# First values ahead of the first keys, and the attention stage's first loads inside the last gate block, in a one-core hybrid attention and RG-LRU layer

## The chip, the core and the metric

The kernel is one program on one core of a Trainium2 chip. The time is the device time of one execution in microseconds (us), from launch to end. The core has five engines that this document names: TensorE (PE; the loading of its stationary operand is PEld), VectorE (DVE), ScalarE (ACT), GpSimd (POOL) and SyncE (SP), on whose queue nearly all DMA transfers are issued. Each engine runs its instructions in the order in which the program gives them; across engines they wait for one another by semaphores. TensorE's granted clock is shown as a share of full speed (1.00 is 2.4 GHz, 0.50 is 1.2 GHz).

## What is computed

One layer: a normalised and modulated input `h` (1152 tokens: 128 of context, 1024 latent) is projected by `w_in`; one part feeds differential attention, the other a recurrence run in both directions; each is gated, and both go through `w_out`. Cut to what matters:

```python
h = rms_norm(x, g_pre) * (1.0 + scale) + shift
p = h @ w_in
q, k, v, g_att, x_lru, g_lru = jnp.split(p, SPLITS, axis=-1)
if use_rope:
    q = axial_rope(q); k = axial_rope(k)
...
o = diff_attention(q, k_all, v_all, lam)          # 8 heads, two softmax maps each
att = (rms_norm(o, g_subln) * (1.0 - lam_init)).reshape(B, T, D_ATT) * jax.nn.silu(g_att)
u = centred_conv(x_lru, conv_w, conv_b)
a_f, b_f = lru_coeffs(u, w_r[0], b_r[0], w_i[0], b_i[0], lru_lam[0])   # two gates: a matmul and a sigmoid each
a_b, b_b = lru_coeffs(u, w_r[1], b_r[1], w_i[1], b_i[1], lru_lam[1])
hf = linear_scan(a_f, b_f, h0_f, False)
hb = linear_scan(a_b, b_b, h0_b, True)
lru = (hf + hb).astype(x.dtype) * jax.nn.silu(g_lru)
out = jnp.concatenate([att, lru], axis=-1) @ w_out
x_new = x + gate * rms_norm(out, g_post)
```

## The kernel before

All matrix work in single precision is done as three matmuls of split operands (`mm3`, lines 117 to 119: high by high, high by low, low by high). So each block of `w_in` is loaded (`wraw`, L257), copied by ScalarE to its high part (`whi`, L266), and GpSimd subtracts to get the low part (`wlo`, L114). `order` lists the blocks in the order of their use; loading and splitting run three blocks ahead of use. `wraw`, `whi` and `wlo` have two buffers each, the latter two for a pair of blocks.

The program has three stages. The **recurrence** goes over eight blocks `n` of 128 channels: projection and convolution, four gate matmuls (`ga<-uh,gwh`), and, one block late, the steps of block `p = n - 1`: `decays`, `gated`, `weights`, `roots` (square roots on ScalarE), `driven`, `scan` (L598, both directions), `both`, `mixed`, `mix_split` (L627 and L114, tiles `lmh` and `lml`), `mix_send` (stores to DRAM, `mix`). Block 7 has no successor, so its steps are put into the next stage.

The **projection stage** goes over four pairs of heads. A query or key block (`qk_block`) is three chunks of 24 matmuls into PSUM tiles, evacuated by ScalarE (L637); then `squares` (ScalarE, L768), `power` (a one-column matmul on TensorE, `un`, L779, and four tiny VectorE steps that make a power of two), `rope` (four VectorE steps, L751 to L754), `halves` (high half on ScalarE L794, low half on VectorE L795) and `send` (stores). A value block (`v_block`) is nine chunks of 24 shorter matmuls; after it `peak` and `spread` find a scale through two TensorE transposes (`vmt`, `vmu`) with VectorE steps between, and `halves` and `send` follow. Between the blocks' chunks `gate_step` sums up the modulation of the output (`gwhs`, `ghl`, and on TensorE `gacc`, L930). PSUM tiles of this kind (`small`) have five buffers. At the end come two gate blocks `g_block` (heads 6 and 7; sigmoid L606, product L612), and the pool `lp` of these stages is closed.

What is put between whose chunks is set by `tick()`, called after each chunk, and `after(d, fn)`, which runs `fn` `d` ticks later. Each `fn` only writes its instructions into the engines' queues at that place.

The **attention stage** runs over 72 tiles of queries (`period`): scores for two maps (`s`), maximum (DVE L1093), exponential (ACT L1103), combination (DVE L1121), transposes by DMA, product with values (`pv`); the matmuls of the output projection (`po<-woh,lt`) are dealt out among the periods by a table. Its first operands are the keys `kt`, queries `qt`, values `vt`, halves of `w_out` (`wor`, cast by `split_wo` to `woh` on ScalarE, L203, and `wol`, L114) and the left sides `lt`, read back from `mix`. Of `w_out` a half has 512 columns, and `GROUPS[0]` are the four rows of blocks 8 to 11.

## Time and profile before

| what | value |
|---|---|
| median of 3 runs | 1281.58 us (1278.58 to 1288.17) |
| the profiled execution, its own time | 1283.49 us |
| its span, first to last instruction | 1281.7 us |
| mean granted TensorE clock | 0.973 |
| busy: PE, PEld | 1174.4 us (92%), 1022.1 us (80%) |
| busy: DVE, ACT, POOL | 990.8 us (77%), 709.2 us (55%), 445.0 us (35%) |

The profile's span leaves out 1.8 us of the execution's time. In the profile's strip of 40 slices TensorE is nearly full up to the attention stage, except in two places, the slices from about 384 to 448 us and the slice from 737 us; the granted clock is below 1.00 in the same places. The recurrence ends at about 397 us, the projection stage at 749 us.

### The profile page before, as it was taken

Reading aid. Unit: us, or ns where it says so; the run is one execution under the profiler, and the core shown is the slowest. Engines: PE = TensorE matmul, PEld = TensorE weight load, DVE = VectorE, ACT = ScalarE, POOL = GpSimd, SP = SyncE. Lnnn points to the kernel's source line nnn. Section 1 sums busy time; section 2 is a strip of 40 time slices with the busy share of each in tenths; the row PEclk is TensorE's granted clock in tenths of the full one; section 3 lists DMA queues with packets and bytes.
Section 4 is the critical chain, followed back from the end, with each engine's and each line's share of the span. In section 5 each row is a group of like instructions: output and inputs, shape, how many; then the busy total and the mean of one; then the engine's idle time right before and its main releaser. Section 6 shows DMA issues by size and latency. Waiting matters only on the chain.

```text
span 1281.7 us, 19990 instructions
## 1 busy us (share of the span) xinstructions
PE 1174.4 (92%) x7704; PEld 1022.1 (80%) x7704; DVE 990.8 (77%) x1420; ACT 709.2 (55%) x1183; POOL 445.0 (35%) x228
## 2 busy tenths in 40 slices
PE   7899999999997899999999959988898887999787
PEld 1499999999997899998999956766666665667676
DVE  5938779777978946856768317899898989999977
ACT  4446545654665233433333327878777786777732
POOL 1421112111202122121122033346865577666724
PEclk8999999999998899999999979999999999999999
DMA  9221322223123634627435174989998988889864
GB/s 369 101 74 41 94 92 80 66 81 114 62 68 104 134 102 128 163 67 170 135 110 126 31 245 93 208 200 229 199 222 186 203 225 183 188 208 210 210 204 164
DMA packets 277815, 188.72 MB, mean 147 GB/s; under 512 B 196172, under 2 KB 246092, under 8 KB 276952
## 3 DMA queue, kind: packets, MB, share of 16 engines
q1 hardware_dynamic: 277432, 186.60, 55.5%
q8 instruction: 60, 0.98, 0.3%
q10 hardware_dynamic: 288, 0.85, 0.2%
q14 instruction: 35, 0.29, 0.1%
HBM read 102.20 MB, written 46.94 MB: 116 GB/s over the span
## 4 chain that ended last, share of the span: by engine, by line
PE 51%; DVE 26%; ACT 6%; DMA 6%; POOL 5%; issue 4%; SPq 1%; DVEq 0%; ACTq 0%; POOLq 0%
DVE mx L1093 5%; DVE e L1121 4%; PE ga L119 3%; PE ga L117 3%; PE ga L118 3%; DMA t<-a 3%; POOL a L1125 3%; PE v L117 3%; PE v L119 3%; PE v L118 3%; PE x L118 2%; PE x L119 2%; PE x L117 2%; PE g L117 2%; PE g L119 2%
## 5 line engine op out<-in xcount | busy, mean ns | idle before, releaser
L114 POOL TENSOR_TENSOR wlo<-wraw,whi 128x1024 fp32r<-128x1024 f32 x48 | 126.2, 2630 | 560.7 <-ACT whi L266 560.7
L1125 POOL TENSOR_TENSOR a<-e,a 128x1152 f16<-128x1152 f32 (+1 forms) x72 | 157.9, 2193 | 172.1 <-ACT a L1124 163.6
L1103 ACT ACTIVATE e<-s,mx,back 128x1152 f32<-128x1152 f32 (+1 forms) x144 | 175.5, 1219 | 67.9 <-DVE fa L1111 18.7
L1093 DVE TENSOR_REDUCE mx<-s 128x1 f32<-128x1152 f32 (+1 forms) x144 | 177.3, 1232 | 37.2 <-PE s L1086 36.5
L1084 PE MATMUL s<-kt,qt 128*128 128x384 f16 (+1 forms) x400 | 88.2, 325 | 41.8 <-ACT e L1103 40.3
L1121 DVE SCALAR_TENSOR_TENSOR e<-e,fa,e 128x1152 f32<-128x1152 f32 (+1 forms) x72 | 113.7, 1579 | 6.4
L117 PE MATMUL po<-woh,lt 128*128 128x512 f32 x216 | 100.1, 463 | 19.2 <-DMA lt<-mix 13.9
L117 PE MATMUL pv<-vt,t 128*128 128x128 f16 x584 | 102.5, 220 | 3.5 <-ACT ot L1140 2.0
L118 PE MATMUL pv<-vt,t 128*128 128x128 f16 x584 | 102.1, 220 | 0.0
L119 PE MATMUL pv<-vt,t 128*128 128x128 f16 x584 | 102.0, 220 | 0.0
L1124 ACT CAST a<-e 128x1152 f16<-128x1152 f32 (+1 forms) x72 | 75.8, 1053 | 36.8 <-DVE e L1121 24.5
L1084 PEld LDWEIGHTS <-qt 128*128 128x128 f16 x400 | 33.5, 97 | 72.1 <-issue 60.7
L1086 PE MATMUL s<-kt,qt 128*128 128x384 f16 (+1 forms) x400 | 87.9, 325 | 0.0
L119 PE MATMUL po<-woh,lt 128*128 128x512 f32 x216 | 87.3, 404 | 0.0
L118 PE MATMUL po<-wol,lt 128*128 128x512 f32 x216 | 87.3, 404 | 0.0
L117 PE MATMUL v<-whi,hTh 128*128 128x256 f32 x288 | 81.8, 284 | 0.0
L119 PE MATMUL v<-whi,hTl 128*128 128x256 f32 x288 | 81.5, 283 | 0.0
L118 PE MATMUL v<-wlo,hTh 128*128 128x256 f32 x288 | 81.5, 283 | 0.0
L117 PEld LDWEIGHTS <-t 128*128 128x128 f16 x584 | 57.3, 98 | 13.9 <-issue 8.9
L117 PEld LDWEIGHTS po<-woh,lt 128*128 128x128 f32 x216 | 42.3, 196 | 32.5 <-issue 14.3
L117 PE MATMUL k<-hTh,whi 128*128 128x384 f32 x192 | 67.4, 351 | 0.0
L117 PE MATMUL x<-hTh,whi 128*128 128x384 f32 x192 | 65.4, 341 | 2.1 <-DVE hTh L400 2.1
(329 smaller groups left out, 3604.7 us busy)
## 6 DMA issues: line engine op xcount, KB each, us to landing
wraw<-in_w_in_dram SPq DMA_DIRECT2D x48, 512.0 KB, 3.6
lt<-mix SPq DMA_DIRECT2D x27, 512.0 KB, 4.5
qs<-hlq SPq DMA_DIRECT2D x64, 144.0 KB, 3.1
qt<-qs SPq DMA_DIRECT2D x72, 128.0 KB, 4.0
wa<-in_w_ada_dram SPq DMA_DIRECT2D x16, 512.0 KB, 7.5
wor<-in_w_out_dram SPq DMA_DIRECT2D x32, 256.0 KB, 5.2
mix<-amo SPq DMA_DIRECT2D x6, 1152.0 KB, 5.1
ks<-hlk SPq DMA_DIRECT2D x32, 160.0 KB, 2.5
```

Source lines behind the costliest of these rows:

```text
L114: eng.tensor_tensor(out=lo, in0=val, in1=f(hi), op=ALU.subtract)
L117: PE.matmul(out, lhsT=lh, rhs=rh, start=start, stop=False)
L118: PE.matmul(out, lhsT=lh, rhs=rl, start=False, stop=False)
L119: PE.matmul(out, lhsT=ll, rhs=rh, start=False, stop=stop)
L1084: PE.matmul(sps[:, j, :w_], lhsT=qt[:, mp], rhs=kt_[:, mp, c], start=True, stop=False)
L1086: PE.matmul(sps[:, j, :w_], lhsT=qt[:, 2 + mp], rhs=kt_[:, mp, c], start=False, stop=True)
L1093: V.tensor_reduce(out=d["mx"][:, mp:mp + 1], in_=sv, axis=AX.XY, op=ALU.max, negate=True)
L1103: S.activation(out=e_[:, :nk].rearrange("p (j c) -> p j c", c=w_), in_=sv, func=AF.Exp, bias=d["mx"][:, mp:mp + 1], scale=unit, accum_out= ...
L1121: V.scalar_tensor_tensor(out=e1, in0=e1, scalar=d["fa"], in1=e0, op0=ALU.mult, op1=ALU.subtract)
L1124: S.copy(out=a16[:, 0:nk], in_=e1)
L1125: G.tensor_tensor(out=a16[:, nk:2 * nk], in0=e1, in1=a16[:, 0:nk], op=ALU.subtract)
```

## The change

Four things are moved; no arithmetic is added or taken away, except that two of the four low parts of each half of `GROUPS[0]` are now subtracted on VectorE in place of GpSimd. (1) In the first pair of heads the value block comes between the two query blocks and the two key blocks, and the weights are loaded in that order. (2) The steps of the recurrence's last block are spread over six ticks in place of four, and the steps of queries 0 and 1 (`squares`, `power` and `rope`, `halves`, `send`) are put at later ticks in the value block. (3) In all later blocks `rope` stands behind `power`, one tick later than before, and so do `halves` and `send`. (4) In the last gate block the loads are put in another order, `w_out`'s first halves are split before that block's sigmoids, and the second halves' loads and the first left side `lt` start there; the `lt` tiles move into the pool `kp`, and `load_lt` is defined earlier.

```diff
+    def load_lt(g, t):
+        lts[g, t] = kp.tile([P, 4, 2, P], F32R, tag="lt", name=f"lt{g}_{t}", bufs=4)
+        src = mixg[g][:, t] if g < 2 else mixg[g][:, :, :, t * P:(t + 1) * P]
+        move(out=lts[g, t].rearrange("p k s c -> p (k s) c"), in_=src.rearrange("p k s c -> p (k s) c"))
...
-            order += [(b + pr, m) for b in (0, 4, 8) for m in range(2)]
+            order += [(b + pr, m) for b in ((0, 4, 8) if pr else (0, 8, 4)) for m in range(2)]
...
         after(1, lambda: (weights(p, 0), weights(p, 1), roots(p)))
-        after(2, lambda: [f_(p, d) for d in range(2) for f_ in (driven, scan)] + [both(p)])
-        after(3, lambda: (mixed(p), mix_split(p), finish_state()))
-        after(4, lambda: mix_send(p))
+        after(2, lambda: (driven(p, 0), scan(p, 0)))
+        after(3, lambda: (driven(p, 1), scan(p, 1)))
+        after(4, lambda: (both(p), mixed(p)))
+        after(5, lambda: (mix_split(p), finish_state()))
+        after(6, lambda: mix_send(p))
...
-                junk = lp.tile([P, T + CTX], F32, tag="gs0" if early else "a", name=f"j{name}")
+                junk = lp.tile([P, T + CTX], F32, tag="a", name=f"j{name}")
...
+            def turned():
+                power()
+                rope(t_, name)
+
             def halves():
-                power()
-                d["hl"] = lp.tile([P, 2, T + CTX], F16, tag="gs2" if early else "w", name=f"hl{name}")
+                d["hl"] = lp.tile([P, 2, T + CTX], F16, tag="w", name=f"hl{name}")
...
-            if first:
-                after(1, lambda: (squares(), rope(t_, name)))
-                after(2, halves)
-                after(3, send)
-                return
-            for j in range(NCH):
-                qk_chunk(which, h, t_, j)
-                tick()
-            squares()
-            if which:
-                after(1, context_keys)
-            rope(t_, name)
-            after(1, halves)
-            after(2, send)
+            steps = [squares, turned, halves, send]
+            if not first:
+                for j in range(NCH):
+                    qk_chunk(which, h, t_, j)
+                    tick()
+            if which or h > 1:
+                squares()
+                if which:
+                    after(1, context_keys)
+                for x, step in enumerate(steps[1:]):
+                    after(1 + x, step)
+            else:
+                for x, step in zip(((7, 8, 10, 11), (8, 10, 12, 13))[h], steps):
+                    after(x - 3 * h, step)
...
         for pr in range(NH // 2):
-            for which in range(2):
-                for m in range(2):
-                    qk_block(which, 2 * pr + m)
-            v_block(pr)
+            for m in range(2):
+                qk_block(0, 2 * pr + m)
+            if pr == 0:
+                v_block(pr)
+            for m in range(2):
+                qk_block(1, 2 * pr + m)
+            if pr:
+                v_block(pr)
...
-        for n in range(4):
+        for n in range(2):
             load_q(n)
+        for kt in GROUPS[0]:
+            load_wo(kt, 0)
+        load_lt(0, 0)
+        after(2, lambda: [split_wo(kt, 0, V if kt % 2 else G) for kt in GROUPS[0][:2]])
+        after(3, lambda: [split_wo(kt, 0, V if kt % 2 else G) for kt in GROUPS[0][2:]])
+        after(3, lambda: [load_wo(kt, 1) for kt in GROUPS[0]])
+        g_block(gp_, NH - 1)
+        for n in range(2, 4):
+            load_q(n)
+        for t in range(1, 3):
+            load_lt(0, t)
         load_v(0)
         for kt in GROUPS[0]:
-            load_wo(kt, 0)
-        for h in range(len(AMONG) + 1, NH):
-            g_block(gp_, h)
-        for half in range(2):
-            for kt in GROUPS[0]:
-                split_wo(kt, half)
-                if half == 0:
-                    load_wo(kt, 1)
+            split_wo(kt, 1, V if kt % 2 else G)
         tick()
```

Three places of the new order matter below. **First**, ScalarE's queue behind the recurrence. Before, the squares of query 0 (`jq`) stand right behind the square roots of block 7 (`w`), and the wait for the power of two (`qksc`) stands in the first `hlq`:

```order
L637 ACTIVATE qfq_3165<-q_0_3166 128x384
L585 ACT_TABLE_LOAD
L585 ACTIVATE w_0_3196<-w_0_3196 128x1158
L585 ACTIVATE w_1_3199<-w_1_3199 128x1158
L768 ACTIVATE jq_3205,sqq_3204<-qfq_3024 128x1152
L637 ACTIVATE qfq_3165<-q_1_3212 128x384
L794 ACTIVATE hlq_3253<-qfq_3024,qksc 128x1152
L637 ACTIVATE qfq_3165<-q_2_3256 128x384
L768 ACTIVATE jq_3298,sqq_3297<-qfq_3165 128x1152
```

In the changed program these squares stand behind the fourth value chunk's copies (`vf<-v_3`); `jq` now takes a buffer that `lmh` had, of which the store must have landed:

```order
L644 ACTIVATE qfq_3165<-q_2_3234 128x384
L858 COPY vf_0_3264<-v_0_3269 128x128
...
L858 COPY vf_0_3264<-v_3_3374 128x128
L858 COPY vf_1_3265<-v_3_3374 128x128
L777 ACTIVATE jq_3404,sqq_3403<-qfq_3024 128x1152
L858 COPY vf_0_3264<-v_4_3406 128x128
L858 COPY vf_1_3265<-v_4_3406 128x128
L273 CAST whi_3300<-wraw_3193 128x1024
L777 ACTIVATE jq_3451,sqq_3450<-qfq_3165 128x1152
```

So six ticks' worth of TensorE work now lies between the roots and these squares. **Second**, ScalarE's queue where a sum of the output's modulation (`gwhs`) is cast for TensorE (`ghl`, read by `gacc`). Before, the cast stands behind the halves of a query (`hlq`), which wait for `rope`'s end on VectorE:

```order
L637 ACTIVATE qfq_4732<-q_0_4733 128x384
L794 ACTIVATE hlq_4773<-qfq_4620,qksc 128x1152
L637 ACTIVATE qfq_4732<-q_1_4776 128x384
L922 CAST ghl_4804<-gwhs_3980 128x512
L637 ACTIVATE qfq_4732<-q_2_4815 128x384
```

In the changed program it stands ahead of them:

```order
L644 ACTIVATE qfq_4727<-q_0_4728 128x384
L644 ACTIVATE qfq_4727<-q_1_4773 128x384
L936 CAST ghl_4801<-gwhs_3975 128x512
L806 ACTIVATE hlq_4804<-qfq_4620,qksc 128x1152
L644 ACTIVATE qfq_4727<-q_2_4807 128x384
```

On VectorE the sums of `gwhs` and the second subtraction of `ghl` likewise stand ahead of `rope` and `hlq`. **Third**, SyncE's queue at the last gate block. Before, four `qt`, `vt` and all eight loads of `w_out` stand ahead of the first left side:

```order
L969 DMA sgs_79<-sg_6268 128x1152
L210 DMA kt_6285<-ks 128x1280 x2
L219 DMA qt_0_6288<-qs_60 128x512
...
L219 DMA qt_3_6294<-qs_60 128x512
L214 DMA vt_6296<-vs_69 128x2560
L196 DMA wor_0_6298<-in_w_out_dram 128x512
...
L196 DMA wor_1_6410<-in_w_out_dram 128x512
L110 DMA lt_0_6442<-mix_81 128x1024
```

In the changed program two `qt` and the four first halves stand ahead of it, and `vt` comes last:

```order
L987 DMA sgs_79<-sg_6268 128x1152
L210 DMA kt_6285<-ks 128x1280 x2
L219 DMA qt_0_6288<-qs_60 128x512
L219 DMA qt_1_6290<-qs_60 128x512
L196 DMA wor_0_6292<-in_w_out_dram 128x512
...
L196 DMA wor_0_6298<-in_w_out_dram 128x512
L110 DMA lt_0_6300<-mix_81 128x1024
L196 DMA wor_1_6393<-in_w_out_dram 128x512
...
L110 DMA lt_2_6414<-mix_81 128x1024
L214 DMA vt_6416<-vs_69 128x2560
```

What moved there is the first left side, past the four second halves, of which each load waits until the split of a first half has freed its buffer.

## Rows read from the trace of the kernel before

**Rows 1.** Two stretches: busy PE, PEld, DVE, ACT, POOL, then clock, DMA share, GB/s.

```profile
480.00:700.00 220.00, 213.97 (x1350) 209.42 (x1349) 153.91 (x241) 79.92 (x141) 43.95 (x16) 0.98 0.50 130
1000.00:1200.00 200.00, 175.59 (x1428) 129.85 (x1427) 186.85 (x283) 149.48 (x281) 138.13 (x71) 0.98 0.90 206
```

**Rows 2.** TensorE's timeline, matmuls after idling: start, length, and [idle <-releaser].

```profile
383.77 0.45 PE L117 MATMUL ga<-uh,gwh 128*128 128x386 f32 x1 [2.12 <-ACT gs L561]
...
411.95 0.59 PE L779 MATMUL unq<-sqq,onesf 128*128 128x1 f32 x2 [6.47 <-ACT jq L768]
427.45 0.59 PE L779 MATMUL unq<-sqq,onesf 128*128 128x1 f32 x2 [4.73 <-ACT jq L768]
...
763.18 0.77 PE L117 MATMUL po<-woh,lt 128*128 128x512 f32 x1 [13.95 <-DMA lt<-mix]
```

**Rows 3.** Stretches around the two waits for `jq`, columns as in rows 1.

```profile
405.50:412.00 6.50, 0.04 (x1) 0.05 (x1) 5.50 (x6) 6.48 (x9) 3.08 (x1) 0.79 0.14 39
412.00:414.00 2.00, 2.00 (x7) 2.00 (x8) 1.97 (x2) 0.28 (x1) 0.00 (x0) 0.50 0.34 139
...
416.00:418.00 2.00, 2.00 (x12) 2.00 (x12) 2.00 (x2) 0.00 (x0) 0.00 (x0) 0.97 0.00 0
...
433.00:434.00 1.00, 1.00 (x7) 1.00 (x6) 1.00 (x1) 0.00 (x0) 0.00 (x0) 0.90 1.36 204
```

**Rows 4.** VectorE's timeline, steps of block 7 and of queries.

```profile
394.93 0.76 DVE L627 CAST lmh<-lsg 128x1152 fp32r<-128x1152 f32 x1
...
406.41 1.37 DVE L577 SCALAR_TENSOR_TENSOR w<-w,gs 128x1158 f32<-128x1158 f32 x1
...
413.19 1.23 DVE L754 TENSOR_TENSOR qfq<-qfq,rsq 128x1024 f32<-128x1024 f32 x1
...
416.07 2.32 DVE L598 TENSOR_TENSOR_SCAN w<-a,vec,gs 128x1024 f32<-128x1024 f32 x1
...
428.55 2.84 DVE L627 CAST lmh<-lsg 128x1152 fp32r<-128x1152 f32 x1
```

**Rows 5.** ScalarE's timeline: squares of query 0; a value chunk's two copies.

```profile
410.66 1.15 ACT L768 ACTIVATE jq<-qfq 128x1152 f32<-128x1152 f32 x1
...
720.77 0.43 ACT L844 COPY vf<-v 128x128 f32<-128x128 f32 x2 [2.45 <-PE v L119]
```

**Rows 6.** Chain that ended last, store of block 6: start, length, what.

```profile
395.72 3.79 DMA mix<-lmh
```

**Rows 7.** GpSimd's timeline: the weight split that the first value chunk will need.

```profile
406.92 3.08 POOL L114 TENSOR_TENSOR wlo<-wraw,whi 128x1024 fp32r<-128x1024 f32 x1 [18.80 <-ACT whi L266]
```

**Rows 8.** TensorE's waits from 480 to 740 us: total, times, longest.

```profile
PE gacc L930 <- ACT ghl L922: 3.5, 2, 2.2
PE gacc L930 <- DVE ghl L114: 1.5, 2, 0.8
```

**Rows 9.** Chain that ended last, transfers ahead of the attention stage.

```profile
738.48 4.59 DMA sgs<-sg
...
746.78 5.67 DMA wor<-in_w_out_dram
...
756.60 6.45 DMA lt<-mix
```

**Rows 10.** ScalarE's timeline, from the last sigmoid to the second tile's exponential.

```profile
749.14 0.49 ACT L606 ACTIVATE sg<-ga 128x384 f32<-128x384 f32 x1 [3.67 <-PE ga L119]
...
758.91 0.62 ACT L203 CAST woh<-wor 128x512 fp32r<-128x512 f32 x1 [0.29 <-DMA wor<-in_w_out_dram]
...
760.84 0.46 ACT L1103 ACTIVATE e<-s,mx,back 128x128 f32<-128x128 f32 x1
...
768.35 0.59 ACT L1044 COPY acc<-po 128x512 f32<-128x512 f32 x1 [6.96 <-PE po L119]
...
771.16 1.32 ACT L1103 ACTIVATE e<-s,mx,back 128x1152 f32<-128x1152 f32 x1 [1.55 <-DVE fa L1111]
```

**Rows 11.** VectorE's timeline: two low parts of `w_out` beside two on GpSimd.

```profile
1215.92 3.37 DVE L114 TENSOR_TENSOR wol<-wor,woh 128x512 fp32r<-128x512 f32 x2
```

More of the change, by code (lines that the diff above doesn't have):

```diff
@@ L219, in load_q @@
         nc.sync.dma_start(out=qts[h, i], in_=qs[h][:, i])
+    lts = {}
+    def load_lt(g, t):
+        lts[g, t] = kp.tile([P, 4, 2, P], F32R, tag="lt", name=f"lt{g}_{t}", bufs=4)
+        src = mixg[g][:, t] if g < 2 else mixg[g][:, :, :, t * P:(t + 1) * P]
+        move(out=lts[g, t].rearrange("p k s c -> p (k s) c"), in_=src.rearrange("p k s c -> p (k s) c"))
     with ExitStack() as pa:
@@ L759, in qk_block @@
             w_ = T + CTX if which else T
-            first, early = (which, h) == (0, 0), (which, h) < (0, 2)
+            first = (which, h) == (0, 0)
             t_ = blk["q0"] if first else lp.tile([P, T + CTX], F32, tag="u", name=f"qf{name}")
@@ L976, in hybrid_step_kernel @@
         kp = ctx.enter_context(tc.tile_pool(name="kp", bufs=2, side="right", reuse_waits="tile"))
-        gp_ = pa.enter_context(tc.tile_pool(name="gp", bufs=2, reuse_waits="tile"))
+        gp_ = pa.enter_context(tc.tile_pool(name="gp", bufs=1, reuse_waits="tile"))
         for n in range(2):
             load_k(0, n)
-        for n in range(4):
+        for n in range(2):
             load_q(n)
+        for kt in GROUPS[0]:
[4 more added lines that the diff above has]
+        after(3, lambda: [load_wo(kt, 1) for kt in GROUPS[0]])
+        assert len(AMONG) + 2 == NH
+        g_block(gp_, NH - 1)
[3 more added lines that the diff above has]
+            load_lt(0, t)
         load_v(0)
         for kt in GROUPS[0]:
-            load_wo(kt, 0)
-        for h in range(len(AMONG) + 1, NH):
-            g_block(gp_, h)
-        for half in range(2):
-            for kt in GROUPS[0]:
-                split_wo(kt, half)
-                if half == 0:
-                    load_wo(kt, 1)
+            split_wo(kt, 1, V if kt % 2 else G)
         tick()
@@ L998, in hybrid_step_kernel @@
         op = pb.enter_context(tc.tile_pool(name="op", bufs=1, reuse_waits="tile"))
-        first_lt = [op.tile([P, 4, 2, P], F32R, tag="lt", name=f"lt0_{t}", bufs=4) for t in range(3)]
         acc_o = [op.tile([P, D], F32, name=f"acc{t}") for t in range(NT)]
@@ L1006, in small @@
             return psb.tile([P, 512], F32, tag=tag, name=name, bufs=1)
-        lts = {}
-        def load_lt(g, t):
-            lts[g, t] = first_lt.pop(0) if first_lt else op.tile([P, 4, 2, P], F32R, tag="lt", name=f"lt{g}_{t}", bufs=4)
-            src = mixg[g][:, t] if g < 2 else mixg[g][:, :, :, t * P:(t + 1) * P]
-            move(out=lts[g, t].rearrange("p k s c -> p (k s) c"), in_=src.rearrange("p k s c -> p (k s) c"))
         def load_lt_pair(ts):
-            tile_ = op.tile([P, 2, 4, P], F32R, tag="lt", name=f"lt3_{ts[0]}", bufs=4)
+            tile_ = kp.tile([P, 2, 4, P], F32R, tag="lt", name=f"lt3_{ts[0]}", bufs=4)
             for a, t in enumerate(ts):
@@ L1278, in hybrid_step_kernel @@
             if i < 3:
-                before(-1, (lambda k=k: load_lt(*k)))
+                assert k == (0, i)
                 continue
```

## Prediction

> **What bounds the kernel now.** I read the strip of 40 slices first: it shows two stages with different limits. Up to the attention stage TensorE is the bound (213.97 of 220 us busy, VectorE 153.91); in the attention stage VectorE is (186.85 of 200), with TensorE idle an eighth of the time and the DMA engines 0.90 busy [rows 1]. So before 749 us the change is worth what it does to TensorE's waits, and afterwards what it does to the moment at which the attention stage starts to flow. Then I listed TensorE's waits by their place. Two long ones stand in the first slices of the projection stage, 6.47 and 4.73 us, both for the squares of a query; one of 13.95 us stands before the first `po` matmul, for a left side `lt` [rows 2]. A third view, the waits of TensorE between them, has only the four for `ghl` of any size, 3.5 and 1.5 us in all [rows 8]. The change touches all three places.
>
> A wait costs more than its length where the clock falls. The granted clock is 0.50 (1.2 GHz) after the 6.47 us wait and back near full only in the stretch from 416 us; after the second wait it rises in the stretch from 433 us [rows 2, 3]. TensorE worked through 4.0 us and some 5.7 us at half clock, which lost 2.0 and 2.9 us. The 2.12 us wait at 383.77 us was followed by matmuls at the usual pace: that matmul is 0.45 us long and those behind it lie 0.17 us apart [rows 2].
>
> **Part one: the queries' squares.** Removed: 6.47 + 4.73 + 2.0 + 2.9 = 16.1 us. The cause was VectorE and ScalarE, which had block 7's steps and both queries' steps at once, while TensorE had only three chunks of work between them. With the value block there, TensorE has nine chunks of 2.88 us (0.43 + 2.45, the distance of two evacuations [rows 5]) before it needs the keys.
>
> What takes its place, step by step:
> - The value block needs the low part of its second weights, which GpSimd has ready at 406.92 + 3.08 = 410.0 us [rows 7]. TensorE comes there at 405.5 us (where it began to wait for `jq`) and one chunk of 4.16 us (0.49 + 3.67 [rows 10]), at 409.7. A wait of 0.3 us.
> - Query 0's squares now stand behind the store of block 7's high part. VectorE ends `weights` at 407.8 [rows 4], waits for the roots, which ScalarE ends where `jq` starts before, at 410.7, the first of them about 1.1 us sooner, and does `driven` and `scan` twice: two times 1.37 + 0.4 + 2.32 (the short scan of the context taken as a sixth of the long one) [rows 4] is 8.2, to 418.3 from 410.1. Then `both` and `mixed` (1.4 each), two pairs of value maxima (an estimate of 0.5 a pair: twice a ninth of a 1.37 us step, and its start), and the cast at 0.76 us: 422.9. The store took 3.79 us in block 6 [rows 6], so it lands at 426.7; the squares take 1.15 and the read of the sum some 0.2 [rows 5]: 428.0. TensorE reaches `un` of query 0 after five value chunks, 410.0 + 14.4 = 424.4. A wait of 3.6 us.
> - `rope` of query 0 (about 5 us, four steps of the size of [rows 4]), `halves` (2.7, a step on ScalarE and one on VectorE) and the same for query 1 follow on VectorE from 428.6, about 8.5 us each with the maxima between, and then the last maxima: 448. TensorE ends the value block and the first key chunk at 428.4 + 11.5 + 4.2 = 444.1 and then wants `vm` for its transpose. A wait of some 3.6 us.
> - The first key's `un` follows the value's two high halves on ScalarE (two steps somewhat longer than `jq`, 2.6) and its own squares: 0.5 us by the same count.
>
> That is 0.3 + 3.6 + 3.6 + 0.5 = 8.0 us, net 16.1 - 8.0 = **8 us gained** if these waits leave the clock at full. They lie between the one that did (2.12) and the ones that did not (4.73), nearer to the latter; each fall would cost 2 to 3 us by the stretches above. So the term is 8, with 2 as the lower end (both fall, and 1 us more of wait) and 14 as the upper (the waits mostly go because a VectorE step or two comes sooner). I take 7, one half of a fall. The lower end has a reason too: the cast took 2.84 us, not 0.76, where a GpSimd split ran beside it [rows 4].
>
> The Trainium skill ("SBUF — State Buffer", the section "SBUF: two separate sides") says that VectorE and GpSimd share one pair of ports as an exclusive lock, so that the later one blocks for the whole instruction. The two casts agree (0.76 alone, 2.84 beside a split). By this rule alone the splits of `w_out` dealt to both engines would take turns; in the last part of the kernel, where they already are, two on VectorE took 3.37 us beside two on GpSimd [rows 11], and with that the term of part three loses under 1 us.
>
> **Part two: the cast of `gwhs`.** TensorE waits 2.2 and 1.3 us for the cast on ScalarE and twice about 0.8 us for the subtraction on VectorE, 5.0 us in all [rows 8]. In the new order the cast stands ahead of the `hlq` that waits for `rope`, and the subtraction ahead of the low half. VectorE's `rope` itself is now behind the sums, so the subtraction comes at about the old time less the two steps that went past it. I take 4 us, bounds 0 and 5. In the same blocks `rope`, `halves` and `send` come one chunk later. VectorE is busy 70% of this stage [rows 1], its steps for a block (about 8 us) fit in the 12.5 us of three chunks, and the tile they read is wanted again only two blocks on: nothing, with the case below as its price if that cover is gone.
>
> **Part three: the start of attention.** Before, `lt` lands after all of SyncE's queue: gate store until 743.1, `w_out`, then `lt` 6.45 us [rows 9]. Now `kt` and two `qt` (2.0 and 0.9 us of issue from 738.85) let the first `wor` go at 741.7. A load lands 5.7 us on by the chain [rows 9], so 747.4; the fourth is issued after the gate store has landed, 743.1, and lands at about 748.8; its cast ends at 749.4 (0.62 [rows 10]). `lt`, right behind, lands at 743.5 + 6.45 = 750.0. The three sigmoids of head 7 now stand behind these four casts: instead of being spread out they run together after 749.4, 1.3 us, and their products, half a microsecond each, end at 751.3, which the first `po` also needs. So TensorE starts `po` at 751.3 in place of 763.18, with a wait of about 2 us, and at full clock its twelve matmuls end at 754.
>
> The attention stage is not held by TensorE, though. The second halves of `w_out` stand on ScalarE ahead of the first exponential, each load waiting for a split: issue 749 to 750.5, landing 3 to 5.7 us later, the last cast over at 754 to 757. From that cast's start to the first exponential's start passed 1.93 us, and from the first `po`'s copy (768.35) to the first full-width exponential 2.81 us (771.16) [rows 10]. The first exponential thus starts at 755.5 to 758, the copy about 0.7 later, and the full-width one follows at 759 to 761.5. Against 771.16 that is 9.7 to 12 us; I take **11**. If the loads come as late as the old ones did behind four `qt` and `vt`, half of it remains (5); if the second halves land in 3 us, 13. The moved `vt` is first needed four periods on. `lt` in another pool has the same four buffers: nothing. What is gained here stays, because the later periods follow each other in a chain.
>
> **Sum.** 7 + 4 + 11 = 22 us. The profiled execution took 1283.49 us, so 1261.5 by its own time; it lies 1.9 us above the median of the runs shown, and from the median, 1281.58, the forecast is **1259.6 us**.
>
> **Rivals.**
> 1. *The new waits are as bad as the old.* Query 0's squares wait for a store, and `vm` for two queries' steps; if the cast meets a split and the clock falls twice, part one gives 1 us and the sum 16: 1265.6. For it speaks that the waits I count are 3.6 us; against, that they are shorter than both that lowered the clock. Chance 0.15. The Trainium skill ("TensorE: Matmul & The Clock Gate", "HAM oscillation — how this bites in real kernels") describes this, an engine that idles again and again and starts at half clock each time; the stretches here agree for 4.73 us and longer.
> 2. *The loads do not begin earlier in effect.* The queue's order changes, but the gate store and the DMA engines hold `wor` and `lt`; the first `po` would start at about 759 and the exponential at 768. Part three gives 3, the sum 14: 1267.6. Against it: `lt`'s 6.45 us counts from an issue that needs no split any more. Chance 0.10. That the change does less still, parts two and three nothing, leaves 7: 1274.6, chance 0.06.
> 3. *Slower: the later `rope` and `halves` hold up the projection stage.* Place: each of the twelve query and key blocks of pairs 1 to 3. VectorE's low half now ends a chunk later, and the block after next needs the tile that it reads; ScalarE would stand at that evacuation and TensorE after five PSUM tiles. It decides where VectorE ends `halves` more than a chunk (4.16 us) behind its place; then each block costs about one wait of 3 us, 36 us in all, against 22 gained: 1295.6. Against it: 30% of idle time on VectorE in this stage [rows 1]. Chance 0.04.
>
> **How the numbers follow.** The forecast case has 0.65; its own range is from 1247 (14 + 5 + 13 = 32 gained, and 2 us for the runs' spread) to 1268 (2 + 0 + 11 gained). Rivals 1 and most of 2 lie inside it. With the two rarer cases left out and a microsecond or two on the upper side, the range is 1248 to 1271. About 1%, 12.8 us, is what a measurement of this kernel can tell from no change. Faster by over 1% means under 1268.8: nearly all of the forecast, rival 1, and half of rival 2, 0.84; within 1% the rest of these and the case of 1274.6, 0.12; slower 0.04.
>
> **What would show it.** In the changed profile: TensorE's waits for `jq` or `vmt` together 5 to 10 us between 397 and 475 us, with no stretch at 0.50; the first query chunk of pair 1 starting at about 470 us in place of 478; no wait of `gacc` over 1 us; the first `po` at about 740 (751.3 less the 11 us gained before it) at clock 1.00, its wait about 2 us; the span of the attention stage as before. The prediction is wrong if VectorE cannot finish block 7 and the queries within the value block, if the second halves of `w_out` land later than 746 on the new time line (757 on the old), or if the attention stage gives the head start back because its DMA traffic, not its chain, sets its pace.

## The result and the profile after

The changed kernel takes 1262.59 us (median of 4 runs, 1259.25 to 1264.33) beside 1281.45 us for the kernel before: ratio 0.984, 95% interval 0.9814 to 0.9866. It ran once more, as a control among the experiments, at 0.9836 (0.9809 to 0.9863). The profiled execution took 1259.25 us with a span of 1257.5, against 1283.49 us before.

TensorE's waits in the first part of the projection stage, of the changed kernel (total, times, longest):

```profile
PE unq L788 <- ACT jq L777: 4.9, 1, 4.9
PE ga L117 <- ACT gs L568: 2.1, 1, 2.1
PE vmt L877 <- DVE vm L870: 1.9, 1, 1.9
PE v L118 <- POOL wlo L114: 0.3, 1, 0.3
```

The two waits for `jq` before [rows 2] are now one, and `vmt` has a wait of its own: 7.1 us without the old one of `ga`, where 11.2 stood. The same view from 470 to 740 us, where four waits of 5.0 us in all for `ghl` were [rows 8], and two of 0.8 us in all for `unk`:

```profile
PE unk L788 <- ACT jk L777: 2.2, 1, 2.2
PE gacc L944 <- DVE ghl L114: 1.2, 1, 1.2
```

Four stretches around the two waits in the value block (columns as in rows 1) answer to [rows 3]:

```profile
424.70:429.60 4.90, 0.02 (x2) 0.02 (x1) 1.84 (x5) 1.33 (x4) 0.00 (x0) 1.00 0.83 233
429.60:433.50 3.90, 3.90 (x20) 3.90 (x21) 3.65 (x9) 2.35 (x5) 2.39 (x1) 0.56 0.05 14
447.30:449.50 2.20, 0.25 (x3) 0.12 (x2) 1.93 (x4) 1.24 (x2) 1.27 (x1) 1.00 0.00 0
449.50:453.50 4.00, 4.00 (x16) 4.00 (x16) 1.11 (x5) 0.00 (x0) 1.39 (x1) 0.61 0.33 107
```

The clock falls behind both, also behind the one of 1.9 us. At 0.56 and 0.61 the two stretches lose 3.90 x 0.44 = 1.7 and 4.00 x 0.39 = 1.6 us.

Why `jq` waits: VectorE's timeline with block 7's two context scans (128 columns) and the cast whose store `jq` waits for ([rows 4] before), GpSimd's split beside it, and `jq` on ScalarE:

```profile
411.38 0.42 DVE L605 TENSOR_TENSOR_SCAN w<-a,gs 128x128 f32<-128x128 f32 x1
...
415.41 2.51 DVE L605 TENSOR_TENSOR_SCAN w<-a,gs 128x128 f32<-128x128 f32 x1
...
423.63 0.75 DVE L634 CAST lmh<-lsg 128x1152 fp32r<-128x1152 f32 x1
...
449.09 0.17 DVE L870 TENSOR_REDUCE vm<-vmx 128x2 f32<-128x20 f32 x1
```

```profile
414.68 2.95 POOL L114 TENSOR_TENSOR wlo<-wraw,whi 128x1024 fp32r<-128x1024 f32 x1 [4.55 <-ACT whi L273]
```

```profile
428.27 1.16 ACT L777 ACTIVATE jq<-qfq 128x1152 f32<-128x1152 f32 x1 [5.98 <-DMA mix<-lmh]
```

The first scan of 128 columns took 0.42 us, the second 2.51, until GpSimd's split was over at 417.63.

The start of the attention stage ([rows 2, 10] before), on TensorE, ScalarE and VectorE in this order:

```profile
740.44 0.73 PE L117 MATMUL po<-woh,lt 128*128 128x512 f32 x1 [2.94 <-DVE sg L619]
...
747.65 1.12 PE L1099 MATMUL s<-kt,qt 128*128 128x384 f16 x3 [2.48 <-ACT e L1118]
```

```profile
743.78 0.62 ACT L203 CAST woh<-wor 128x512 fp32r<-128x512 f32 x1 [0.51 <-DMA wor<-in_w_out_dram]
...
747.06 0.46 ACT L1118 ACTIVATE e<-s,mx,back 128x128 f32<-128x128 f32 x1
...
747.51 0.57 ACT L1059 COPY acc<-po 128x512 f32<-128x512 f32 x1
...
751.53 1.32 ACT L1118 ACTIVATE e<-s,mx,back 128x1152 f32<-128x1152 f32 x1 [3.00 <-DVE fa L1126]
```

```profile
744.43 0.74 DVE L114 TENSOR_TENSOR wol<-wor,woh 128x512 fp32r<-128x512 f32 x1 [1.90 <-ACT woh L203]
745.09 0.28 DVE L1108 TENSOR_REDUCE mx<-s 128x1 f32<-128x128 f32 x1
```

The clock under these `po` matmuls (a stretch, columns as in rows 1):

```profile
740.00:744.00 4.00, 3.56 (x9) 2.82 (x10) 2.08 (x4) 2.09 (x4) 1.94 (x2) 0.57 0.75 235
```

The wait of 13.95 us for `lt` is gone; 2.94 us for the last gate product stand there. Behind it the clock is 0.57. The first maximum follows VectorE's last subtraction for the second `w_out` halves, and the first full-width exponential comes at 751.53 in place of 771.16.

### The profile page after: what moved, and what is told of

Its sections match the earlier page's. It is cut to its first block, busy times and chain, and to the rows that moved or that the text cites. A ratio compares the mean times of both kernels' runs of the same rounds, so it can differ in the third digit from the quotient of the medians.

```text
span 1257.5 us, 19998 instructions
## 1 busy us (share of the span) xinstructions
PE 1166.2 (93%) x7704; PEld 1016.0 (81%) x7704; DVE 979.8 (78%) x1424; ACT 709.3 (56%) x1183; POOL 439.3 (35%) x224
## 4 chain that ended last, share of the span: by engine, by line
PE 55%; DVE 23%; ACT 6%; POOL 5%; DMA 5%; issue 4%; SPq 1%; DVEq 0%; ACTq 0%; POOLq 0%
DVE mx L1108 6%; DVE e L1136 4%; PE ga L119 3%; PE ga L117 3%; PE ga L118 3%; POOL a L1140 3%; PE x L118 2%; PE x L119 2%; PE x L117 2%; PE g L119 2%; PE k L117 2%; PE g L117 2%; PE g L118 2%; PE k L119 2%; PE k L118 2%
## 5 line engine op out<-in xcount | busy, mean ns | idle before, releaser
L114 POOL TENSOR_TENSOR wlo<-wraw,whi 128x1024 fp32r<-128x1024 f32 x48 | 123.1, 2566 | 552.0 <-ACT whi L273 552.0
L1108 DVE TENSOR_REDUCE mx<-s 128x1 f32<-128x1152 f32 (+1 forms) x144 | 177.4, 1232 | 21.8 <-PE s L1101 20.8
L117 PE MATMUL po<-woh,lt 128*128 128x512 f32 x216 | 98.4, 456 | 8.1 <-DVE acc L1065 3.3
L119 PE MATMUL po<-woh,lt 128*128 128x512 f32 x216 | 86.1, 398 | 0.0
L118 PE MATMUL x<-hTl,whi 128*128 128x384 f32 x192 | 65.3, 340 | 1.7 <-DVE hTl L114 0.9
```

The costliest lines, as they stand in the source:

```text
L114: eng.tensor_tensor(out=lo, in0=val, in1=f(hi), op=ALU.subtract)
L117: PE.matmul(out, lhsT=lh, rhs=rh, start=start, stop=False)
L118: PE.matmul(out, lhsT=lh, rhs=rl, start=False, stop=False)
L119: PE.matmul(out, lhsT=ll, rhs=rh, start=False, stop=stop)
L1108: V.tensor_reduce(out=d["mx"][:, mp:mp + 1], in_=sv, axis=AX.XY, op=ALU.max, negate=True)
```

## The experiments

Eleven kernels and the control. Two marks were read from each profile: the start of the last gate matmul (end of the projection stage) and of the first full-width exponential (attention flows); the last column is the time from there to the 126th such exponential. A third mark takes out how far an execution has come when it reaches the part that was edited: the matmul behind the 2.12 us wait for `gs` [rows 2], which stands ahead of all edits and comes between 383.77 and 386.96 us in these profiles. The fourth column is the time from it to the last gate matmul.

| kernel | ratio to before, 95% | last `ga` | from the wait for `gs` | first wide `e` | to the 126th |
|---|---|---|---|---|---|
| before | 1 | 748.76 | 364.99 | 771.16 | 425.26 |
| changed | 0.984 (0.9814 to 0.9866) | 737.04 | 353.19 | 751.53 | 420.43 |
| control: changed again | 0.9836 (0.9809 to 0.9863) | 738.41 | 353.46 | 752.83 | 427.23 |
| start put back | 0.9934 (0.9919 to 0.9949) | 741.80 | 356.56 | 763.55 | 425.22 |
| rope put back | 0.9873 (0.9856 to 0.989) | 742.89 | 357.75 | 757.23 | 424.27 |
| order put back | 0.9884 (0.9857 to 0.9911) | 744.72 | 360.31 | 758.86 | 428.10 |
| start alone | 0.9916 (0.9894 to 0.9937) | 750.57 | 365.14 | 764.48 | 424.14 |
| splits late | 0.9889 (0.9864 to 0.9914) | 738.21 | 353.16 | 755.50 | 425.22 |
| own buffer | 0.9799 (0.978 to 0.9818) | 734.74 | 347.91 | 748.77 | 420.53 |
| own buffer, peak late | 0.9757 (0.9735 to 0.978) | 729.30 | 343.90 | 742.64 | 421.96 |
| compact | 0.9822 (0.9799 to 0.9845) | 737.46 | 353.55 | 750.95 | 422.68 |
| compact, own buffer, peak late | 0.9755 (0.9737 to 0.9773) | 730.83 | 343.87 | 744.09 | 420.50 |
| second halves late | 0.9853 (0.9829 to 0.9876) | 737.18 | 353.14 | 747.17 | 424.48 |
| all mends | 0.9787 (0.9765 to 0.9809) | 729.19 | 343.89 | 741.84 | 429.26 |

A difference of two ratios counts in microseconds of 1282; the changed kernel is taken at 0.9838, the mean of its two. With intervals of 0.002 to 0.003 on either side, a difference is uncertain by 3 to 4 us. The fourth column is finer: it lies between 353.14 and 353.55 in the five profiles whose projection stage has the same edits or differs by the compact form alone, and between 343.87 and 343.90 in the three with both mends. It holds each profile's chance clock falls too, and says nothing of what comes behind it.

**Control.** 

> The changed kernel without an edit, beside the others on the same chip, so that differences of a few us can be told. Its ratio to the kernel before was 0.984 with an interval of 0.005; every theory expects the same, 0.984.

It came out so, by the ratio. The profiled execution is the longest of its five (1267.33 us, the others 1258.98 to 1260.84), and the marks put its excess behind the first wide exponential: 427.23 us to the 126th, 420.43 in the other profile of this kernel.

**Start put back.** The hunks on the attention start reversed (with them the gate blocks' pool, which has one buffer in place of two in the changed kernel).

> The changed kernel with the attention start put back as it was before the change (w_out, queries and left sides loaded behind one another, splits behind the last gate block); parts one and two stay. Forecast's term for part three, 11 us: 1262.6 + 11 = 1273.6 us. By the profile after, in which the first full-width exponential came 19.6 us earlier of which 11.7 already at the last gate matmul, the part is worth 7.9: 1270.5. Rival (attention is bound by its own flow and a later start is caught up there): under 1265.

0.9934, so by the ratio part three is worth 0.0096 x 1282 = 12.3 us, and attention does not catch up. The wait is back, on TensorE's timeline:

```profile
531.27 0.59 PE L781 MATMUL unk<-sqk,onesf 128*128 128x1 f32 x2 [2.21 <-ACT jk L770]
...
755.80 0.77 PE L117 MATMUL po<-woh,lt 128*128 128x512 f32 x1 [13.54 <-DMA lt<-mix]
```

The first of these rows is another matter: the changed kernel has the same wait of 2.21 us, with the same work around it, and in its two profiles the clock stayed. First the stretch of this kernel behind the wait, then that of the changed one:

```profile
530.00:536.00 6.00, 4.73 (x22) 4.73 (x23) 5.46 (x13) 2.65 (x6) 2.88 (x1) 0.59 0.63 153
```

```profile
530.00:535.00 5.00, 5.00 (x45) 5.00 (x44) 4.83 (x11) 1.21 (x4) 2.90 (x1) 1.00 0.60 142
```

From the wait for `gs` to the last gate matmul this kernel takes 3.1 to 3.4 us longer, and that is what the fall costs (3.4 us, worked out further down); an execution may or may not have it. From the last gate matmul to the first wide exponential it takes 21.75 us, the changed kernel 14.49 and 14.42: 7.3 us are the start itself.

**Rope put back.**

```diff
-                for x, step in enumerate(steps[1:]):
-                    after(1 + x, step)
+                rope(t_, name)
+                after(1, lambda: (power(), halves()))
+                after(2, send)
```

> The changed kernel with rope ahead of power again in the later blocks, halves one tick and send two ticks behind the squares as before; everything else as changed. Forecast's term for part two, 4 us: 1266.6, and the gate sums' matmul (gacc) waits for VectorE again for some 5 us where the profile after has 1.2. By what is left of the 11.7 us at the projections' end after the 5.0 up to the third queries, 6.7: 1269.3. Rival (the gate sums wait for something else and rope's place is no matter): 1261.5 to 1263.5.

0.0035 x 1282 = 4.5 us, as forecast, and 4.3 to 4.6 from the wait for `gs` to the last gate matmul. The waits are those of before, in the view from 470 to 745 us:

```profile
PE gacc L945 <- ACT ghl L937: 3.5, 2, 2.2
PE gacc L945 <- DVE ghl L114: 1.6, 2, 0.8
PE unk L788 <- ACT jk L777: 0.5, 1, 0.5
```

With `rope` ahead, `unk` does not wait: the change traded 2.2 us there for the gate sums. This profile has one clock fall behind the gate sums (0.50 from 582 to 584 us), the kernel before two.

**Order put back.** Pair 0 in the order queries, keys, values, its steps at the old ticks and in the old buffers, the recurrence's rest in three ticks.

> The changed kernel with the first value block behind the first keys again, the first two queries' steps at their old ticks, and the recurrence's rest in its three old ticks; the later blocks' rope and the attention start stay changed. Forecast's term for part one, 7 us: 1269.6. By the profile after, 5.0 us at the third queries' start: 1267.6. Rival (the two clock falls in the value block eat what the order gains): 1263.6.

0.0046 x 1282 = 5.9 us, between the two figures that were expected, with runs that scatter from 1263.07 to 1274.86 us. The profiled one took 1274.42. From the wait for `gs` to the last gate matmul it needs 6.9 to 7.1 us more, of which 6.00 x 0.28 = 1.7 are a fall from 535 to 541 us (clock 0.72) behind the 2.2 us wait for `jk`; the changed kernel's profiles have none there.

**Start alone.** The kernel before with only the hunks on the start.

> The kernel before with the attention start of the change alone. If the parts add up, it gains what its undoing cost, 11.4 us at the first full-width exponential (of that about 8 behind the last gate matmul, the rest a clock fall that not every execution has): ratio 0.991 to 0.994. Rival (the start is only worth something behind a faster projection stage): 0.997 to 1.000.

0.0084 x 1282 = 10.8 us, as expected. Its projection stage ends as late as before (750.57), yet the way to the first wide exponential is 13.91 us in place of 22.40. The start needs no faster projections. The waits of the projection stage are all there, the start's is not (views up to 480 and from 480 us):

```profile
PE unq L786 <- ACT jq L775: 11.1, 2, 6.5
```

```profile
PE gacc L937 <- ACT ghl L929: 3.5, 2, 2.2
PE po L117 <- DVE sg L619: 2.0, 1, 2.0
```

**Splits late.** The loads of the first halves and of the left sides as changed, the splits of the first halves behind the last gate block.

```diff
-        after(2, lambda: [split_wo(kt, 0, V if kt % 2 else G) for kt in GROUPS[0][:2]])
-        after(3, lambda: [split_wo(kt, 0, V if kt % 2 else G) for kt in GROUPS[0][2:]])
-        after(3, lambda: [load_wo(kt, 1) for kt in GROUPS[0]])
...
-        for kt in GROUPS[0]:
-            split_wo(kt, 1, V if kt % 2 else G)
+        for half in range(2):
+            for kt in GROUPS[0]:
+                split_wo(kt, half, V if kt % 2 else G)
+                if half == 0:
+                    load_wo(kt, 1)
```

> The changed kernel with its loads where the change has them but the splits of the first w_out halves back behind the last gate block, ahead of those of the second halves (and so the second halves' loads too). If the earlier loads carry part three (the first w_out matmul waited 13.95 us for a left side's load before), most of it stays: the first w_out matmul waits some 3 to 6 us in all, the first full-width exponential comes 3 to 5 us later than in the changed kernel, ratio to the kernel before 0.986 to 0.988. Rival (the splits' place carries it): near the kernel with the whole start put back, 0.992 to 0.994.

0.9889, between the two and a little over the upper end: 6.5 us lost of part three's 10.8 to 12.3. The first wide exponential is only 2.7 to 4.0 us later, and the wait has moved from `po` to the second tile's scores (view of TensorE's waits from 480 us):

```profile
PE s L1099 <- ACT e L1118: 6.1, 1, 6.1
...
PE po L117 <- ACT woh L203: 1.0, 1, 1.0
```

By the marks the loads carry most of the start, as expected: from the last gate matmul to the first wide exponential 17.29 us, where the changed kernel has 14.4 to 14.5 and the old start 21.75 to 22.40. By the time the splits' place carries half. The uncertainty of 3 to 4 us covers the gap between the two. The second halves' loads came later here too, so their share and that of the splits are not told apart.

**Own buffer.**

```diff
-                junk = lp.tile([P, T + CTX], F32, tag="a", name=f"j{name}")
+                junk = lp.tile([P, w_], F32, tag="a" if which or h > 1 else "xp", name=f"j{name}")
```

> The changed kernel with one edit: the first two queries' squares write their unused elementwise result to another buffer, which no store reads, so that they don't wait for the store of the recurrence's last result. If that store is what holds the matmul of the first queries' sum of squares (4.9 us wait, then about 3 us at the 1.2 GHz clock, worth 1.5 to 2), the wait falls under 1 us and the time goes to 1256 to 1257.5. Rival (ScalarE or VectorE is late there whatever the buffer, or the next wait grows by as much): 1260.5 to 1263.

0.0039 x 1282 = 5.0 us, as expected; 5.3 to 5.6 from the wait for `gs` to the last gate matmul. In the view of TensorE's waits up to 480 us the one for `jq` is gone, and the rival's remark holds in part, since the next wait grew from 1.9 to 3.4:

```profile
PE vmt L877 <- DVE vm L870: 3.4, 1, 3.4
PE ga L117 <- ACT gs L568: 2.1, 1, 2.1
PE v L118 <- POOL wlo L114: 0.3, 1, 0.3
```

**Own buffer, peak late.** The same and

```diff
-            after(1, peak)
-            after(2, spread)
-            after(3, halves)
-            after(4, send)
+            for x, step in enumerate((peak, spread, halves, send)):
+                after(1 + x + (pr == 0), step)
```

> The changed kernel with the first two queries' unused squares in another buffer, and the first value block's four last steps (peak, spread, halves, send) one tick later each. The wait that is left in the value block's wake (the peak's transpose for VectorE's maximum, 3.4 us with the buffer's edit alone, with one clock fall behind it, a mean of 0.75 and 0.91 over 10 us, worth 1.7) should go: 5 us less than the buffer's edit alone, ratio about 0.976 to the kernel before. Rival (VectorE is late anyway, and the keys' matmuls or the next queries' squares wait for it instead): no gain on the buffer's edit, 0.980.

0.9757: 5.4 us more by the ratio, 4.0 up to the last gate matmul, and the best version together with the compact one. In two stretches where the falls were (columns as in rows 1), TensorE is busy without a gap at full clock:

```profile
424.00:434.00 10.00, 10.00 (x86) 10.00 (x86) 9.79 (x21) 4.40 (x11) 2.41 (x1) 1.00 0.61 172
446.00:456.00 10.00, 10.00 (x60) 9.60 (x59) 1.31 (x7) 3.87 (x7) 3.50 (x2) 1.00 0.76 164
```

The two mends brought 10.4 us by the ratios and 8.9 to 10.2 at the first wide exponential. The waits were 6.8 us and the falls 3.3, together 10.1; a wait of 1.0 us for the first `unk` is new, which leaves 9.1, and 9.3 to 9.6 were gained from the wait for `gs` to the last gate matmul.

**Compact.** The hunk on the recurrence's rest reversed.

> The changed kernel with the recurrence's rest in three ticks as before the change (both scans and their weights in one tick), all else as changed. If the spread is what makes the store of the recurrence's last result so late that the first queries' squares wait for it, the 4.9 us wait falls and the time to about 1257 to 1259 (ratio 0.980 to 0.982). Rival (the steps in a lump hold VectorE and ScalarE, and the value block's matmuls wait for a free PSUM buffer or a later step): 1 to 5 us slower than the changed kernel, 0.985 to 0.988.

0.9822, 2.1 us under the changed kernel, which the intervals can't tell from nothing. Both expectations failed in what they expected of the waits: the one for `jq` is 4.7 us still, and no other has grown. Behind the roots VectorE was busy almost without a gap in the changed kernel already, so the steps come at the same time in either form; the store leaves at 424.34 (424.40 in the changed kernel). VectorE's second short scan meets the split here too, and `jq` starts as late (VectorE's and ScalarE's timelines):

```profile
415.88 2.54 DVE L605 TENSOR_TENSOR_SCAN w<-a,gs 128x128 f32<-128x128 f32 x1
```

```profile
429.12 1.16 ACT L775 ACTIVATE jq<-qfq 128x1152 f32<-128x1152 f32 x1 [5.77 <-DMA mix<-lmh]
```

**Compact, own buffer, peak late.** All three edits.

> The two mends of the value block with the recurrence's rest in three ticks as before the change. With the squares no longer behind the store, the spread has nothing left to hold up: if it is worth nothing in itself, 0.975 to 0.978, as with the two mends. Rival (in a lump VectorE's scans make the value block's or the queries' steps late): 2 to 5 us slower, 0.978 to 0.981.

0.9755 beside 0.9757, and 343.87 beside 343.90 us up to the last gate matmul: the spread is worth nothing there.

**Second halves late.**

```diff
-        for kt in GROUPS[0]:
-            split_wo(kt, 1, V if kt % 2 else G)
...
+        for x, kt in enumerate(GROUPS[0]):
+            at_period(x // 2, lambda kt=kt: split_wo(kt, 1))
```

> The changed kernel with the splits of the second w_out halves in the first two periods of attention, their subtractions on GpSimd, not ahead of the first maximum. If these splits hold the first maximum and with it the first exponentials (VectorE's last subtraction ended at 745.2, the first maximum followed at once, its scores had been done since 738), the first full-width exponential comes about 3 us earlier (748.5 against 751.5): 3 us under the changed kernel. Rival (the first scores of the second tile follow the w_out matmuls, not the maximum, or attention gives the gain back): within 1 us of the changed kernel.

0.9853, no gain: my reading of what held the first exponentials was right, and nothing of it was left in the time. On ScalarE's timeline the first wide exponential starts 4.4 us sooner:

```profile
747.17 1.31 ACT L1116 ACTIVATE e<-s,mx,back 128x1152 f32<-128x1152 f32 x1 [0.53 <-DVE fa L1124]
```

But the eleventh comes at 779.31 against 781.68, 2.4 us sooner, and the 101st at 1088.28 against 1088.63. The first ten steps are where a loss can be told from scatter: from the first to the eleventh wide exponential all twelve profiles without the late splits take 30.07 to 30.45 us, this one 32.14. The rest of the way scatters by more than what is left. One place where it is given back is VectorE's first full combination, 2.21 us beside GpSimd's subtraction, 1.42 in the changed kernel:

```profile
753.98 2.21 DVE L1134 SCALAR_TENSOR_TENSOR e<-e,fa,e 128x1152 f32<-128x1152 f32 x1
```

**All mends.** Own buffer, peak late and second halves late together.

> The changed kernel with both mends of the value block (own buffer for the unused squares, peak and what follows a tick later) and the second halves' splits in the first periods of attention. The splits alone moved the first full-width exponential 4.4 us forward and left the time as it was, so the time should be that of the two mends, ratio 0.974 to 0.977, with the first full-width exponential at 738 to 739. Rival (the gain was there and hidden by scatter in attention): 0.972 to 0.973.

0.9787, 3.8 us over the two mends, about as much as the uncertainty; the ratio lies outside both expectations, its interval reaches into the first. The first wide exponential starts at 741.84, not at 738 to 739, 0.8 us sooner than with the two mends, and ten further on it is 2.7 us behind (775.50 against 772.76): 33.66 us for the first ten. The late casts stand on ScalarE ahead of the copy that frees `po`, whose wait is 3.4 us in all against 1.8 with the two mends (waits from 480 us):

```profile
PE po L117 <- ACT acc L1055: 3.4, 2, 2.9
```

## Why the prediction was right, step by step

The forecast was 1259.6 us, 3.0 under the measured median; by the profiled execution 1261.5 against 1259.25. Its terms 7, 4 and 11 came out at 5.9, 4.5 and 10.8 to 12.3 us in the runs that undo or do one part. Their sum, 21 to 23 us, is the 0.0162 x 1282 = 20.8 us of the whole within the intervals. The marks say it more finely. Up to the last gate matmul 11.7 us were gained against 7 + 4 forecast, but between it and the first wide exponential 7.9, not 11. That the profiled execution still came in under the forecast is luck: its stretch to the 126th exponential is 4.8 us shorter than before, which the forecast did not have, and in the control it is 2.0 us longer.

*Part one.* The mechanism held: each of the new waits stands where the working put it, at 0.3, 4.9 and 1.9 us against 0.3, 3.6 and 3.6, and the last (0.5) did not come: 7.1 in all against 8.0. The third is short because the second held TensorE back: with the second gone it is 3.4. The wait for the store was longer because the working took both short scans at 0.4 us and counted no split beside them; the second took 2.51. The cast itself, for which that fear was stated, met none (0.75). The step that failed is the clock. I took half a fall, from a 2.12 us wait that had left it alone, and named "no stretch at 0.50" as what would show the case right. There were two falls, 3.3 us. The premise was one execution's: behind that same wait of 2.12 us, with the same instructions, the clock falls in three of the fourteen profiles (order put back, compact, second halves late; in the compact one 0.60 from 385.5 to 389.5 us). Net that is 16.1 - 7.1 - 3.3 = 5.7; the first query chunk of pair 1 starts at 473.00, 5.0 us before 478 and not at 470. So rival 1 was half right: the falls came, the waits in all did not grow.

*Part two.* 4 us forecast, 4.5 measured, with two errors of opposite sign. `gacc`'s waits fell from 5.0 to 1.2 us. I missed the falls behind them: the kernel before has two, in stretches around 586 and 682 us, and the changed kernel none. Of before:

```profile
580.00:595.00 15.00, 12.03 (x60) 11.34 (x60) 13.25 (x21) 5.73 (x9) 3.23 (x1) 0.89 0.90 250
678.00:690.00 12.00, 9.91 (x49) 9.19 (x48) 10.32 (x14) 6.00 (x10) 3.10 (x1) 0.86 0.71 134
```

They lost 15 x 0.11 + 12 x 0.14 = 3.3 us, and they are chance in part: with `rope` put back only one of the two came. On the other side is the 2.2 us wait of `unk`, which the working did not have. Rival 3 is there in small: with `rope` put back `unk` waits 0.5 us, so the later steps cost 1.7 us at one place, where the rival had 3 at each of twelve.

*Part three.* The first `po` was forecast at about 740 and came at 740.44; the last cast over by 743 to 746 and came at 744.4. The wait was 2.9 us, not 2, and the clock fell where 1.00 was forecast: the `po` and the second tile's scores ran in stretches at 0.57 and 0.66. The wide exponential was due at 748 to 750.5 on the new time line (759 to 761.5 less 11) and came at 751.53. What was mis-sized are the two spacings taken from before [rows 10]. From the last cast's start to the first exponential 3.28 us passed, not 1.93: VectorE's last subtraction and the first maximum now stand between them. From the first copy to the wide exponential it was 4.02, not 2.81: the second tile's first three scores took 1.12 us at the lowered clock, and waited 2.48 us for the first exponential. Together that is 2.6 us. Rival 2 fell with the first `po`. Of the term's 11 us, 7.3 to 8.5 lie behind the last gate matmul by the marks; what the runs with the start alone or put back show above that is within their uncertainty, and the clock fall at 530 us that the run with the start put back had.

*"What is gained here stays"* did hold for the change in its first ten exponentials (30.15 us, before 30.26) and in its time, and not for the late second halves, where 4.4 us at the first wide exponential gave none at the end. Why was shown only in part: the late splits put ScalarE and GpSimd work into the first periods, and cost 2 to 3.5 us in the first ten exponentials.

## What to carry to other kernels

A buffer that an operation writes for nothing is still a dependency: here it tied a sum of squares to the landing of a store, and cost about 5 us where the reordering around it gained about 6. When a reordering leaves a bubble of two microseconds, move the step that waits one chunk on; price the wait with its possible clock fall, and check with a run whether an earlier start of the next stage is still there at its end. An edit of a few microseconds is told better from marks inside the trace, counted from one that stands ahead of the edit, than from the time of the whole: here such a stretch repeated within 0.4 us where the time scattered by 5.

## What had not been expected of the hardware

**The clock after short waits.** Waits of TensorE of about 2 us are followed by stretches at half clock (the 1.2 GHz level) in some executions and not in others, with the same instructions. The 2.21 us wait for `jk` kept 1.00 in the changed kernel's two profiles and was followed by 0.59 with the start put back and by 0.72 (535 to 541 us) with the order put back; the 1.9 us wait for `vm` was followed by 0.61 in the changed kernel and not in the compact one (1.00 from 451 to 457 us), where the wait for `gs` was. Beside the wait itself a fall costs 1.6 us (the stretch at 0.61) to 3.4 us (6.00 x 0.41 in the one at 0.59, and 4.00 x 0.24 in the four microseconds behind it, at 0.76). The Trainium skill ("TensorE: Matmul & The Clock Gate", "HAM oscillation — how this bites in real kernels") tells of the fall after waits on loads; the trace agrees for the 4.9 us wait, which was for a store. For the waits of 2 us no run here shows what decides.

**Small VectorE steps beside GpSimd.** The changed kernel's two profiles differ by 6.8 us between the first and the 126th wide exponential. Of that, 3.9 us lie between the 41st and the 61st (66.31 against 70.18 us), where the clock is 1.00 in both, and two steps alone are longer by as much: 2.86 - 0.76 and 2.17 - 0.16, together 4.1 (others there are longer or shorter by up to 0.8). VectorE and GpSimd in the control:

```profile
911.46 2.86 DVE L1136 SCALAR_TENSOR_TENSOR e<-e,fa,e 128x128 f32<-128x128 f32 x1
...
920.96 1.36 DVE L1108 TENSOR_REDUCE mx<-s 128x1 f32<-128x1152 f32 x1
...
940.29 2.17 DVE L174 TENSOR_TENSOR tt<-y 128x9 f32<-128x9 f32 x1
```

```profile
911.52 2.66 POOL L114 TENSOR_TENSOR amo<-sga,amo 128x1152 fp32r<-128x1152 f32 x1
...
920.65 2.37 POOL L1140 TENSOR_TENSOR a<-e,a 128x1152 f16<-128x1152 f32 x1 [4.82 <-ACT a L1139]
...
940.04 2.39 POOL L1140 TENSOR_TENSOR a<-e,a 128x1152 f16<-128x1152 f32 x1 [3.00 <-ACT a L1139]
```

The same two steps in the changed kernel's first profile:

```profile
909.30 0.76 DVE L1136 SCALAR_TENSOR_TENSOR e<-e,fa,e 128x128 f32<-128x128 f32 x1
...
936.38 0.16 DVE L174 TENSOR_TENSOR tt<-y 128x9 f32<-128x9 f32 x1
```

A step of nine columns a partition takes 2.17 us when it begins inside GpSimd's 2.39; the step of 128 columns ended with GpSimd's 2.66 (it began 0.06 us ahead of it by the profile, too close to tell the order). Not every step is held: a maximum over 1152 columns, which reads one tensor, the scores in PSUM, took its usual 1.36 us inside GpSimd's 2.37. The Trainium skill ("SBUF — State Buffer", "SBUF: two separate sides") has the two engines share a pair of ports as an exclusive lock for a whole instruction, on VectorE's side for steps with two inputs in SBUF or in a mode that uses both ports; these rows and the short scan (0.42 and 2.51) agree. So what a small VectorE step with two tensor inputs costs depends on what GpSimd does at its start, and an edit of 2 us can be hidden or doubled by where the steps fall; that may be why differences of 2 us between the times of these kernels did not settle, which no run here shows.
